# Attention's values of two groups by seven products of quarters, in a two-layer block on one core

## The chip, the cores and the metric

The kernel runs on one core of one Trainium2 chip. The metric is the device time of one execution, in microseconds (us); the lower the better. TensorE's matmul side is called PE here, its loading of the stationary operand PEld, VectorE DVE, ScalarE ACT, GpSimd POOL and SyncE SP.

## The reference: what is computed

Two layers run on 512 tokens of width 1024, in fp32. Layer 0 mixes tokens by a gated linear recurrence (HGRN2), layer 1 by dilated attention, and each ends in a feed-forward network (FFN). The change touches layer 1's attention. Its core in the reference:

```python
proj = (u @ w_in).reshape(B, S, N_GROUPS, 3, ATT_HEADS, ATT_HEAD_DIM)
for gi, (window, dilation) in enumerate(((128, 1), (512, 4), (2048, 16))):
    q = apply_partial_rope(proj[:, :, gi, 0], cos, sin) * scale
    k = apply_partial_rope(proj[:, :, gi, 1], cos, sin)
    v = proj[:, :, gi, 2]
    o_g, lse_g = dilated_group_attention(q, k, v, window, dilation)
```

Three groups of eight heads of 128 have their own queries, keys and values, each a product of u (512 x 1024) with 1024 columns of the weights; the three outputs are merged by a softmax over their log-sums. Group 1 attends in token order; groups 2 and 3 (1 and 2 in the code, which counts from 0) attend inside the four classes of tokens that are equal modulo four.

## The kernel before, in words

**Precision.** An fp32 value is kept as two fp32r parts, hi and lo (`uh`, `ul` for u; `hi`, `lo` or `hiq`, `loq` for weights). A product is three matmuls, hi by hi, lo by hi, hi by lo, issued by `three` (lines 408 to 410 of the kernel before, 428 to 430 of the changed one). Weights come from DRAM as fp32 in tiles `raw` of 128 x 2048 (1 MB), two at a time, on SP's queue; ACT casts a tile to hi (line 83), DVE subtracts to get lo (line 84). Three pairs of hi and lo exist. `Stream` holds the list of all loads of the program in the order of their use; the kernel's loops take from it in that order, and `weave` mixes in the loads of the adaptive-norm weights (`ada`), which DVE multiplies and sums (line 244).

**FFN.** It computes its products by seven products of quarters instead of eight. For these `token_sums` makes sums of token quarters (`th`, `tl`), POOL and DVE make sums of weight quarters (lines 772, 776, 780), and DVE combines the products out of PSUM (lines 817 to 832). Its matmuls have 256 columns.

**Attention.** `tok_proj` computes the values of one group and half of the columns (512): for each of four tiles of 128 tokens, eight tiles of 128 of the inner dimension, three matmuls of 512 columns, u stationary and the weights moving, 96 in all. For groups 2 and 3 the stationary tile takes each fourth token of u (`res`), so that V stands by classes. `block` computes queries or keys of one head and group with the weights stationary and all 512 tokens of u moving (24 matmuls of 512 columns); ACT evacuates them (`qk_evac`, line 1554), for groups 2 and 3 sorted into classes on the way, and copies the 32 rows that turn into `turning` (1555); DVE turns them (`turn_pair`, lines 1562 to 1565), ACT copies them back (1568), with a step for groups 2 and 3. Group 1's first half of values runs inside the FFN of layer 0 (`v_prod`), where it fills PE while the residual h and u are made. Then come groups 2 and 3, the pairs of heads 0 to 4, the second half of the values of all groups, and the pairs of heads 5 to 7. The softmax work of a head (`scores`, `merge`, `flip`, `pv`) is put at fixed numbers of blocks behind its pairs; `mixer_out` holds what is left of the last heads in its `tail`.

## Time and profile before

| | |
|---|---|
| median of 3 runs | 1522.97 us (1522.70 to 1523.41) |
| the profiled execution | 1522.93 us |
| its span, first to last instruction | 1521.0 us |
[...]
| busy: PE, DVE, ACT, POOL | 1506.4, 1024.8, 689.5, 234.9 us |
| DRAM read, written | 189.17 MB, 2.16 MB |

A profile shows one execution. Matmuls overlap, so what one of them costs is read from the distance between the starts of neighbours in the timeline, not from its length. "A <- B" in a wait reads: A waited, and B's end let it go. A line number is that of the helper that issued the instruction where a helper did.

### The profile page before, as it was taken

Reading aid. Unit: us, or ns where it says so; the run is one execution under the profiler, and the core shown is the slowest. Engines: PE = TensorE matmul, PEld = TensorE weight load, DVE = VectorE, ACT = ScalarE, POOL = GpSimd, SP = SyncE. Lnnn points to the kernel's source line nnn. Section 1 sums busy time; section 2 is a strip of 40 time slices with the busy share of each in tenths; the row PEclk is TensorE's granted clock in tenths of the full one; section 3 lists DMA queues with packets and bytes.
Section 4 is the critical chain, followed back from the end, with each engine's and each line's share of the span. In section 5 each row is a group of like instructions: output and inputs, shape, how many; then the busy total and the mean of one; then the engine's idle time right before and its main releaser. Section 6 shows DMA issues by size and latency. Waiting matters only on the chain.

```text
span 1521.0 us, 22710 instructions
## 1 busy us (share of the span) xinstructions
PE 1506.4 (99%) x8943; PEld 1325.7 (87%) x8943; DVE 1024.8 (67%) x1750; ACT 689.5 (45%) x1099; POOL 234.9 (15%) x208
## 2 busy tenths in 40 slices
PE   8999999999999999999999999999999999999998
PEld 6777888898999988889888888988888899999886
DVE  4587867487888897472567686335656978888633
ACT  4443433353444432362456664245645544544231
POOL 1011211031222212040010111000002212221100
PEclk9999999999999999999999999999999999999999
DMA  9654445125333366414544433433212333334521
GB/s 308 185 160 147 150 133 166 56 89 161 112 111 112 111 201 223 137 56 138 167 117 131 120 110 108 150 100 90 78 32 80 100 96 112 109 105 148 199 106 56
DMA packets 205498, 192.79 MB, mean 127 GB/s; under 512 B 6680, under 2 KB 164560, under 8 KB 205392
## 3 DMA queue, kind: packets, MB, share of 16 engines
q1 hardware_dynamic: 203856, 190.87, 40.9%
q8 instruction: 70, 1.15, 0.3%
q0 software_dynamic: 1024, 0.13, 0.2%
q10 hardware_dynamic: 512, 0.35, 0.1%
q14 instruction: 36, 0.29, 0.1%
HBM read 189.17 MB, written 2.16 MB: 126 GB/s over the span
## 4 chain that ended last, share of the span: by engine, by line
PE 93%; issue 2%; ACT 2%; POOL 1%; DVE 1%; DMA 1%; POOLq 0%; DVEq 0%; ACTq 0%
PE ps_mm L408 21%; PE ps_mm L410 20%; PE ps_mm L409 20%; PE ps_b L408 3%; PE ps_b L410 3%; PE ps_b L409 3%; PE ps_a L408 3%; PE ps_a L409 3%; PE ps_a L410 3%; PE ps_mm L1162 1%; ACT junk L444 1%; PE ps_a L1162 1%; PE ps_a L1607 1%; PE ps_a L1589 1%; PE ps_mm L222 1%
## 5 line engine op out<-in xcount | busy, mean ns | idle before, releaser
L408 PE MATMUL ps_mm<-uh,hi 128*128 128x512 f32 (+1 forms) x784 | 297.1, 379 | 0.0
L409 PE MATMUL ps_mm<-ul,hi 128*128 128x512 f32 (+1 forms) x784 | 294.9, 376 | 1.0 <-DVE ul L508 1.0
L410 PE MATMUL ps_mm<-uh,lo 128*128 128x512 f32 (+1 forms) x784 | 295.9, 377 | 0.0
L84 DVE TENSOR_TENSOR lo<-raw,hi 128x2048 fp32r<-128x2048 f32 x76 | 180.4, 2374 | 163.7 <-ACT hi L83 163.6
L83 ACT CAST hi<-raw 128x2048 fp32r<-128x2048 f32 x76 | 145.1, 1909 | 161.1 <-DMA raw<-in_ffn_w_out_dram 45.8
L408 PEld LDWEIGHTS ps_mm<-uh,hi 128*128 128x128 f32 x784 | 147.7, 188 | 34.2 <-issue 8.4
L409 PEld LDWEIGHTS ps_mm<-ul,hi 128*128 128x128 f32 x784 | 147.7, 188 | 26.4 <-DVE ul L508 1.4
L410 PEld LDWEIGHTS ps_mm<-uh,lo 128*128 128x128 f32 x784 | 147.6, 188 | 25.9
L788 ACT CAST hiq<-raw 128x1024 fp32r<-128x1024 f32 x68 | 68.3, 1050 | 65.7 <-DVE raw L776 64.7
L408 PE MATMUL ps_mm<-hi,oh 128*128 128x512 f32 x240 | 94.0, 392 | 0.0
L409 PE MATMUL ps_mm<-lo,oh 128*128 128x512 f32 x240 | 93.4, 389 | 0.0
L246 POOL PARTITION_ALL_REDUCE shared<-shared x14 | 46.4, 3312 | 281.3 <-DVE shared L244 281.2
L244 DVE SCALAR_TENSOR_TENSOR shared<-raw,cond,shared 128x512 f32<-128x512 f32 x98 | 73.2, 747 | 21.4 <-DMA raw<-in_ada_w_dram 19.9
L792 DVE TENSOR_TENSOR loq<-raw,hiq 128x1024 fp32r<-128x1024 f32 x68 | 80.0, 1217 | 0.4 <-ACT hiq L788 0.4
L410 PE MATMUL ps_mm<-hi,ul 128*128 128x512 f32 x192 | 75.9, 395 | 0.0
L409 PE MATMUL ps_mm<-lo,uh 128*128 128x512 f32 x192 | 75.9, 395 | 0.0
L408 PE MATMUL ps_mm<-hi,uh 128*128 128x512 f32 x192 | 74.5, 396 | 0.0
L772 POOL TENSOR_TENSOR raw<-raw 128x512 f32<-128x512 f32 x34 | 54.6, 1605 | 104.2 <-DVE loq L768 47.7
L410 PE MATMUL ps_mm<-hi,ol 128*128 128x512 f32 x176 | 68.5, 389 | 0.0
L776 DVE TENSOR_TENSOR raw<-raw 128x1024 f32<-128x1024 f32 x34 | 41.7, 1225 | 39.1 <-POOL raw L772 39.1
L408 PE MATMUL ps_a<-hi,oh 128*128 128x512 f32 x152 | 59.6, 392 | 0.0
L409 PE MATMUL ps_a<-lo,oh 128*128 128x512 f32 x152 | 59.2, 389 | 0.0
(402 smaller groups left out, 3813.3 us busy)
## 6 DMA issues: line engine op xcount, KB each, us to landing
raw<-in_ada_w_dram SPq DMA_DIRECT2D x40, 1024.0 KB, 5.2
raw<-in_ffn_w_in_dram SPq DMA_DIRECT2D x136, 256.0 KB, 4.3
raw<-in_attn_w_in_dram SPq DMA_DIRECT2D x48, 512.0 KB, 5.2
raw<-in_ffn_w_out_dram SPq DMA_DIRECT2D x22, 1024.0 KB, 4.9
raw<-in_hgrn_w_in_dram SPq DMA_DIRECT2D x12, 1024.0 KB, 5.5
raw<-in_attn_w_in_dram SPq DMA_DIRECT2D x12, 1024.0 KB, 5.1
raw<-in_ffn_w_in_dram SPq DMA_DIRECT2D x10, 1024.0 KB, 5.4
first<-in_ada_w_dram SPq DMA_DIRECT2D x14, 512.0 KB, 7.5
```

The source lines that it names most:

```text
L83: self.nc.scalar.copy(hi, t)
L84: self.nc.vector.tensor_sub(lo, t, hi.bitcast(F32))
L244: dve.scalar_tensor_tensor(a, r[:, k], sc, a, op0=OP.mult, op1=OP.add)
L246: pool.partition_all_reduce(a, a, P, bass.bass_isa.ReduceOp.add)
L408: pe.matmul(ps, ah, bh, start=start, stop=False)
L409: pe.matmul(ps, ah, bl, start=False, stop=False)
L410: pe.matmul(ps, al, bh, start=False, stop=stop)
L772: pool.tensor_add(r[:, 2], r[:, 2], r[:, 0])
L776: dve.tensor_tensor(r[:, 0:2], r[:, 0:3:2], r[:, 1:2].broadcast_to((P, 2, 512)), op=OP.add)
L788: act.copy(hi, src)
L792: dve.tensor_sub(lo, src, hi.bitcast(F32))
L1162: pe.matmul(vbanks[hf, t], a, w, start=e == 0 and which == 0, stop=e == KT - 1 and which == 2)
```

## The change

**Values.** Groups 2 and 3 use `seven_values`. A half of a group's columns is a product of 512 tokens x 1024 with 1024 x 512; it is cut into quarters (tokens, inner dimension and columns in two), and seven products of 256 tokens x 512 x 256 replace eight. Each product is two tiles of tokens x four inner tiles x three matmuls of 256 columns, 24; seven make 168. Four of them take sums or differences of u's quarters (`th`, `tl`), four sums or differences of the weights' quarters, which POOL (line 1389) and DVE (1390 to 1392) make in the raw tiles; ACT casts each quarter (1371), DVE subtracts (1372). ACT copies the first product into V (1418), DVE combines the other six (1426 to 1440). `prepare` steps the next group's weights while the present group's products run.

**u by classes.** u's two parts are also kept in the order of classes (`apart`, eight casts on ACT, line 1651, eight on DVE, 1652). Queries and keys use them, so that their evacuation is in place for groups 2 and 3 and has a step for group 1; the angles' table is sorted likewise. `th` and `tl` lie in the place of `uh` and `ul`, which nobody needs after group 1's values.

**Order.** Group 1's second half of values follows the first directly; it goes to DRAM (`v_away`) and comes back into V[0] after the second block of seven products. Then the pairs of group 1 and 2 of head 0, the first block (groups 2 and 3, first half), the third pair, heads 1 to 4, the second block, heads 5 to 7.

**Room.** The residual h goes to DRAM (`h_away`, 4 x 512 KB, at the end of FFN of layer 0, on ACT's queue) and comes back in `mixer_out`'s tail; its place holds the sums of tokens at first and then the softmax tiles `PN`, `PR` and `pt`. There is one tile `turning`, not two. The masks are made earlier, in V's room. The diff, cut:

```diff
-        at = []
-        order = []
-        for hd in range(NH):
-            if hd == 0:
-                for g in range(3):
-                    order.append(("v", g, 0))
-                    at += av(g, 0)
-            for g in range(3):
+        order, at = [], []
+        def values(hf, gs):
+            for g in gs:
+                order.append(("v", g, hf))
+                at.extend([("half", w[1]) for w in av(g, hf)])
+        def pairs(hd, gs=range(3)):
+            for g in gs:
                 order.append(("qk", g, hd))
                 at.append(aqk(g, hd))
-            if hd == 4:
-                for g in range(3):
-                    order.append(("v", g, 1))
-                    at += av(g, 1)
-        items += weave(at, ada_seq((1, 2), (1, 4), (1, 3)), 6, 2)
+        def woven(others, every):
+            items.extend(weave(at, others, 0, every))
+            at.clear()
+        for hf in range(2):
+            at += av(0, hf)
+        pairs(0, (0, 1))
+        values(0, (1, 2))
+        woven([], 1)
+        late = ada_seq((1, 2), (1, 4), (1, 3))
+        pairs(0, (2,))
+        for hd in range(1, 5):
+            pairs(hd)
+        woven(late[:8], 1.5)
+        values(1, (1, 2))
+        woven([], 1)
+        for hd in range(5, NH):
+            pairs(hd)
+        woven(late[8:], 1.3)
...
+                    for t in range(NT):
+                        act.dma_start(h_away[t], h[:, t])
...
-        def tok_proj(dst, c0, view, ticks=()):
+        def tok_proj(done):
             ws = [st.take(), st.take(1)]
             for t in range(NT):
                 ps = bank("mm")
+                tok = slice(t * P, (t + 1) * P)
                 for kt in range(KT):
                     whi, wlo = ws[kt // 4]
                     w = slice((kt % 4) * 512, (kt % 4 + 1) * 512)
-                    three(ps, view(uh[:, kt])[t], view(ul[:, kt])[t], whi[:, w], wlo[:, w], kt == 0, kt == KT - 1)
-                act.copy(dst[:, t, c0:c0 + 512], ps)
-                if t in ticks:
-                    fl.tick()
-        nat = lambda a: [a[:, t * P:(t + 1) * P] for t in range(NT)]
-        res = lambda a: [a.rearrange("p (l r) -> p r l", r=4)[:, t] for t in range(NT)]
...
+        def seven_values(dsts, apart, th, tl):
+            C = lambda raw, c: V4(raw)[:, :, c * 256:c * 256 + 256]
+            G = lambda t, o: V4(t[:, o * 1024:(o + 1) * 1024])
+            u_of = lambda r, c: lambda kt, n: [a[:, r * 4 + kt, c * 256 + n * P:c * 256 + (n + 1) * P] for a in apart]
+            t_of = lambda i: lambda kt, n: [a[:, i, kt, n * P:(n + 1) * P] for a in (th, tl)]
+            raws, tiles = {}, {}
+            def cut(i, tile, o, k, c):
+                hi, lo = tiles[i, tile]
+                src = C(raws[i][k], c)
+                act.copy(G(hi, o), src)
+                dve.tensor_sub(G(lo, o), src, G(hi, o).bitcast(F32))
+            def place(i, tile):
+                tiles[i, tile] = st.part_tiles()
+            def prepare(i, step):
+                if i >= len(dsts):
+                    return
+                if step == 0:
+                    raws[i] = [st.whole(), st.whole()]
+                    place(i, 0)
+                    cut(i, 0, 0, 0, 0)
+                    cut(i, 0, 1, 1, 1)
+                elif step == 1:
+                    place(i, 1)
+                    cut(i, 1, 0, 1, 0)
+                    a, b = raws[i]
+                    pool.tensor_add(C(b, 1), C(b, 1), C(a, 1))
+                    dve.tensor_add(C(a, 1), C(a, 1), C(a, 0))
+                    dve.tensor_add(C(a, 0), C(a, 0), C(b, 1))
+                    dve.tensor_add(C(b, 0), C(b, 0), C(a, 0))
+                    cut(i, 1, 1, 0, 0)
+                elif step == 2:
+                    place(i, 2)
+                    cut(i, 2, 1, 0, 1)
+                    cut(i, 2, 0, 1, 1)
+                else:
+                    place(i, 3)
+                    cut(i, 3, 0, 1, 0)
+                    raws.pop(i)
+                    st.fill()
+            def run(ps, i, tile, o, us):
+                hi, lo = tiles[i, tile]
+                for n in range(2):
+                    for kt in range(4):
+                        w = slice(o * 1024 + kt * 256, o * 1024 + (kt + 1) * 256)
+                        three(ps[:, n * 256:(n + 1) * 256], *us(kt, n), hi[:, w], lo[:, w], kt == 0, kt == 3)
+            H2 = lambda a: a.rearrange("p (n c) -> p n c", n=2)
+            for step in range(3):
+                prepare(0, step)
+            for i, dst in enumerate(dsts):
+                X, Y, Z, U = (dst[:, t:t + 2, c:c + 256] for c in (0, 256) for t in (0, 2))
+                m1 = bank("mm")
+                run(m1, i, 0, 0, u_of(0, 0))
+                act.copy(X, H2(m1))
+                m4 = bank("a")
+                run(m4, i, 0, 1, t_of(2))
+                prepare(i, 3)
+                m2 = bank("mm")
+                run(m2, i, 1, 0, u_of(1, 0))
+                m6 = bank("mm")
+                run(m6, i, 1, 1, t_of(3))
+                dve.tensor_add(Y, X, H2(m6))
+                dve.tensor_add(X, X, H2(m2))
+                prepare(i + 1, 0)
+                m5 = bank("mm")
+                run(m5, i, 2, 0, t_of(0))
+                m7 = bank("mm")
+                run(m7, i, 2, 1, t_of(1))
+                dve.scalar_tensor_tensor(Z, Y, -1.0, H2(m7), op0=OP.mult, op1=OP.subtract)
+                dve.tensor_add(Y, Y, H2(m5))
+                dve.tensor_sub(U, Z, H2(m5))
+                dve.tensor_sub(Z, Z, H2(m4))
+                prepare(i + 1, 1)
+                m3 = bank("mm")
+                run(m3, i, 3, 0, u_of(1, 1))
+                dve.tensor_add(Y, Y, H2(m3))
+                prepare(i + 1, 2)
...
+        def to_away(t, ps):
+            act.copy(V[1][:, t], ps)
+            if t == NT - 1:
+                act.dma_start(v_away, V[1])
...
+        PNs, PR_h = [h[:, k].rearrange("p (t n) -> p t n", t=4) for k in range(2)], h[:, 2].rearrange("p (t n) -> p t n", t=4)
...
+        apart = [up.tile([P, KT, S], F32R, name=f"apart{k}") for k in range(2)]
+        for kt in range(KT):
+            act.copy(V4(apart[0][:, kt]), L4(uh[:, kt]).bitcast(F32))
+            dve.tensor_copy(V4(apart[1][:, kt]), L4(ul[:, kt]).bitcast(F32))
+        tok_proj(to_away)
+        th, tl = (t.rearrange("p (a b) n -> p a (b n)", a=4).rearrange("p a (b n) -> p a b n", b=4) for t in (uh, ul))
+        token_sums(th, tl, h.rearrange("p t (a n) -> p (t a) n", a=2), *apart)()
...
-                pair.append(fresh(mk, [64, S], "turning", 2))
-            act.activation(*((tl, ps) if g == 0 else (V4(tl), L4(ps))), AF.Copy, scale=scale)
+                pair.append(fresh(mk, [64, S], "turning", 1))
+            act.activation(*((tl.rearrange("p (l r) -> p l r", r=4), R4(ps)) if g == 0 else (tl, ps)), AF.Copy, scale=scale)
...
-                act.copy(*((dst, src) if g == 0 else (V4(dst), L4(src))))
+                act.copy(*((dst.rearrange("p (l r) -> p l r", r=4), R4(src)) if g == 0 else (dst, src)))
...
-        for kind, g, i in order[1:]:
+        for kind, g, i in order:
             if kind == "v":
-                tok_proj(V[g], 0, nat if g == 0 else res, (0, 1, 2) if i and g == 0 else ())
+                if g == 1:
+                    seven_values(V[1:], apart, th, tl)
+                    if i:
+                        act.dma_start(V[0], v_away)
                 continue
...
-                ps = block(whi, wlo, k * D, P)
+                ps = block(whi, wlo, k * D, P, u=apart)
...
-        tail = {-1: [lambda: scores(7, 2), mkx.close], 2: [lambda: merge_r(7)], 3: [lambda: merge_n(7)],
-                4: [lambda: flips_r(7)], 5: [lambda: pv_r(7), lambda: flips_n(7)], 6: [lambda: pv_n(7)]}
+        upx.close()
+        tail = {-1: [lambda: scores(7, 2), mkx.close], 2: [lambda: merge_r(7), back(0)], 3: [lambda: merge_n(7)],
+                4: [lambda: flips_r(7)], 5: [lambda: pv_r(7), lambda: flips_n(7), back(2)], 6: [lambda: pv_n(7), back(1)],
+                7: [back(3)]}
```

Three places show how instructions move. First ACT, where the attention begins; `V` is the evacuated values, hi tiles the weights. Before:

```order
L104 CAST hi_6205<-raw_5815 128x1024 x2
L1522 COPY V_6089<-ps_mm_6213 128x512
L83 CAST hi_6297<-raw_5985 128x2048
L1522 COPY V_6089<-ps_mm_6239 128x512
L83 CAST hi_6303<-raw_6211 128x2048
L1334 COPY V_6090<-ps_mm_6310 128x512
```

Now, the casts into `apart` and the residual's DMAs stand between the last cast for group 1's first half and the evacuation of its last tiles:

```order
L105 CAST hi_6206<-raw_5816 128x1024 x2
L1050 DMA h_away<-h 128x1024 x4
L1651 CAST apart_6286<-uh 128x512 x8
L1626 COPY V_6090<-ps_mm_6219 128x512
L84 CAST hi_6304<-raw_5986 128x2048
L1626 COPY V_6090<-ps_mm_6245 128x512
L84 CAST hi_6311<-raw_6212 128x2048
```

What moved: the second tile of the next projection's weights (`hi_6304`) is cast behind eight more casts.

Second DVE, where it prepares weights for values. Before, at the first values of groups 2 and 3, each tile of weights is one subtraction, with adaptive-norm work between:

```order
L84 TENSOR_TENSOR lo_6298<-raw_5985,hi_6297 128x2048
L84 TENSOR_TENSOR lo_6304<-raw_6211,hi_6303 128x2048
L84 TENSOR_TENSOR lo_6415<-raw_6301,hi_6414 128x2048
L84 TENSOR_TENSOR lo_6421<-raw_6307,hi_6420 128x2048
L242 TENSOR_SCALAR shared<-raw_6418,cond 128x512
```

Now, in the first block, for group 3's sums of weights (`raw_6605`, `raw_6684` are its two raw tiles) among group 2's last combinations:

```order
L1440 TENSOR_TENSOR V_6091<-V_6091,ps_mm_6811 128x2x256
L1390 TENSOR_TENSOR raw_6605<-raw_6605 128x4x256
L1436 TENSOR_TENSOR V_6091<-V_6091,ps_a_6655 128x2x256
L1372 TENSOR_TENSOR loq_6838<-raw_6684,hiq_6837 128x1024
L1391 TENSOR_TENSOR raw_6605<-raw_6605,raw_6684 128x4x256
L1372 TENSOR_TENSOR loq_6838<-raw_6605,hiq_6837 128x1024
L1392 TENSOR_TENSOR raw_6684<-raw_6684,raw_6605 128x4x256
L1372 TENSOR_TENSOR loq_6802<-raw_6605,hiq_6801 128x1024
```

What moved: three sums of raw quarters and the subtractions that depend on them stand in one queue with the combinations.

Third POOL, at the end of layer 0's FFN; `rr` is the power that gives the root of the norm, which u of a token tile waits for. Before, the masks stand behind all of u; here from the fourth tile's root on:

```order
L459 TENSOR_TENSOR rr_6008<-rv_6006,expo 128x1
L459 TENSOR_TENSOR rr_6041<-rv_6039,expo 128x1
L508 TENSOR_TENSOR ul<-u_6029,uh 128x4x128
L508 TENSOR_TENSOR ul<-u_6034,uh 128x4x128
L459 TENSOR_TENSOR rr_6070<-rv_6068,expo 128x1
L459 TENSOR_TENSOR rr_6137<-rv_6135,expo 128x1
L508 TENSOR_TENSOR ul<-u_6139,uh 128x4x128
L508 TENSOR_TENSOR ul<-u_6144,uh 128x4x128
L508 TENSOR_TENSOR ul<-u_6191,uh 128x4x128
L508 TENSOR_TENSOR ul<-u_6196,uh 128x4x128
L1534 MEMSET zero 128x128
L1540 IOTA lq 128x128
L1535 AFFINE_SELECT maskN<-zero 128x128
L1538 AFFINE_SELECT maskN<-zero 128x128
L1538 AFFINE_SELECT maskR<-zero 128x128
```

Now:

```order
L479 TENSOR_TENSOR rr_6009<-rv_6007,expo 128x1
L1658 MEMSET V_6092 128x128
L1663 IOTA V_6092 128x128
L1659 AFFINE_SELECT maskN<-V_6092 128x128
L1662 AFFINE_SELECT maskN<-V_6092 128x128
L1662 AFFINE_SELECT maskR<-V_6092 128x128
L479 TENSOR_TENSOR rr_6042<-rv_6040,expo 128x1
L528 TENSOR_TENSOR ul<-u_6030,uh 128x4x128
```

What moved: the five operations of the masks stand before the root of the third token tile (`rr_6042`).

## Rows read from the trace of the kernel before

**Rows 1.** The page's first part: busy time of each engine, share of the span, instructions

```profile
PE 1506.4 (99%) x8943; PEld 1325.7 (87%) x8943; DVE 1024.8 (67%) x1750; ACT 689.5 (45%) x1099; POOL 234.9 (15%) x208
```

**Rows 2.** Waits of PE in the attention: engine, line, releaser; total us, times, longest

```profile
PE ps_b L1691 <- ACT pt L1660: 1.7, 1, 1.7
```

**Rows 3.** Stretch, us, busy us (and count) of PE, PEld, DVE, ACT, POOL; clock, DMA share

```profile
700.00:727.00 27.00, 27.00 (x116) 27.00 (x116) 7.32 (x6) 8.27 (x8) 0.00 (x0) 1.00 0.41 117
800.00:900.00 100.00, 100.00 (x533) 85.89 (x533) 74.89 (x230) 64.43 (x112) 13.44 (x13) 1.00 0.44 122
```

**Rows 4.** Timeline of PE, strided values: start, length, line, operation, out<-in

```profile
700.50 0.39 PE L408 MATMUL ps_mm<-hi,uh 128*128 128x512 f32 x1
...
723.06 0.39 PE L408 MATMUL ps_mm<-hi,uh 128*128 128x512 f32 x1
```

**Rows 5.** Timeline of PE in the second FFN, matmuls of 256 columns

```profile
1243.15 0.28 PE L408 MATMUL ps_mm<-th,hiq 128*128 128x256 f32 x1
...
1246.55 0.28 PE L408 MATMUL ps_mm<-th,hiq 128*128 128x256 f32 x1
...
1246.89 0.28 PE L408 MATMUL ps_mm<-uh,hiq 128*128 128x256 f32 x1
...
1249.51 0.28 PE L409 MATMUL ps_a<-ul,hiq 128*128 128x256 f32 x1
```

**Rows 6.** Groups of stationary loads (PEld), whole span: busy us, mean ns | idle

```profile
L410 PEld LDWEIGHTS ps_mm<-hi,ul 128*128 128x128 f32 x192 | 51.6, 269 | 2.5
...
L408 PEld LDWEIGHTS ps_mm<-th,hiq 128*128 128x128 f32 x204 | 38.4, 188 | 0.0
```

**Rows 7.** Timelines of ACT and of PE at the start of the attention

```profile
674.34 2.00 ACT L104 CAST hi<-raw 128x1024 fp32r<-128x1024 f32 x2
...
683.34 0.40 PE L409 MATMUL ps_mm<-lo,uh 128*128 128x512 f32 x1
```

**Rows 8.** Timeline of ACT at the last heads

```profile
1116.56 1.08 ACT L1683 COPY oT_late<-ps_b 128x512 f32<-128x512 f32 x1 [2.73 <-PE ps_b L1682]
1117.67 2.24 ACT L1568 COPY qk<-turning 32x512 f32<-32x512 f32 x2
```

**Rows 9.** Groups of instructions in the second FFN, 1190 to 1400

```profile
L792 DVE TENSOR_TENSOR loq<-raw,hiq 128x1024 fp32r<-128x1024 f32 x36 | 42.3, 1217 | 0.0
L788 ACT CAST hiq<-raw 128x1024 fp32r<-128x1024 f32 x36 | 36.2, 1050 | 32.5 <-DVE raw L776 31.7 <-DVE raw L780 0.8
L772 POOL TENSOR_TENSOR raw<-raw 128x512 f32<-128x512 f32 x18 | 29.4, 1631 | 56.2 <-DVE loq L768 27.5 <-DVE spare L768 15.1 <-DMA raw<-in_ffn_w_in_dram 13.6
...
L776 DVE TENSOR_TENSOR raw<-raw 128x1024 f32<-128x1024 f32 x18 | 22.0, 1225 | 19.7 <-POOL raw L772 19.7
...
L821 DVE TENSOR_TENSOR shared<-shared,ps_a 128x512 f32<-128x512 f32 x9 | 6.1, 680 | 0.6 <-ACT shared L861 0.6
```

**Rows 10.** Timelines of POOL and of DVE around the masks

```profile
662.05 0.55 POOL L459 TENSOR_TENSOR rr<-rv,expo 128x1 f32<-128x1 f32 x1 [3.00 <-DVE rv L457]
...
676.60 0.20 POOL L1534 MEMSET zero<- 128x128 f32 x1
...
677.74 1.26 POOL L1538 TENSOR_SCALAR_AFFINE_SELECT maskN<-zero 128x128 f32<-128x128 f32 x1
678.96 0.29 POOL L1538 TENSOR_SCALAR_AFFINE_SELECT maskR<-zero 128x128 f32<-128x128 f32 x1
...
675.42 3.43 DVE L105 TENSOR_TENSOR lo<-raw,hi 128x1024 fp32r<-128x1024 f32 x2 [1.92 <-ACT hi L104]
```

**Rows 11.** DMA issues in the attention: count, KB each, median us to landing

```profile
raw<-in_attn_w_in_dram SPq DMA_DIRECT2D x48, 512.0 KB, 5.2
...
raw<-in_attn_w_in_dram SPq DMA_DIRECT2D x9, 1024.0 KB, 5.1
```

**Rows 12.** Groups of instructions in the attention, 655 to 1160

```profile
L84 DVE TENSOR_TENSOR lo<-raw,hi 128x2048 fp32r<-128x2048 f32 x35 | 82.2, 2348 | 106.6 <-ACT hi L83 106.6
...
L1568 ACT COPY qk<-turning 32x512 f32<-32x512 f32 x48 | 45.3, 944 | 25.8 <-DVE turning L1565 22.5 <-DVE wZ L1633 2.7
```

46 lines of the change are left out of this document (27 added, 19 removed).

## The prediction

> **What bounds the kernel now.** I read the busy times first: TensorE (PE) is busy for 1506.4 of 1521.0 us, the next engine, VectorE (DVE), for 1024.8 [rows 1]. Then PE's waits in the attention: one only, 1.7 us [rows 2]. Then the stretches: while the strided value projections run (700 to 727) PE is full and DVE has 7.32 us of work in 27; while the query/key pairs run (800 to 900) PE is full and DVE has 74.89 in 100, ScalarE (ACT) 64.43 [rows 3]. So time falls only if PE gets less to do, and only as far as what feeds it keeps up. The profiled execution took 1522.93 us, its span of 1521.0 and 1.93 around it; the median of the runs, 1522.97, is 0.04 from it, so I work against 1522.93.
>
> **The change, part by part.** *The products.* Now four value projections (groups 2 and 3, two halves of columns) issue 96 matmuls of 512 columns each, with tokens read at a step of four as the stationary side. Two of these matmuls, 96 apart, start at 700.50 and 723.06 [rows 4]: 22.56 / 96 = 0.2350 us each. All: 4 x 96 x 0.2350 = 90.2 us. After it, each projection is 7 products x 24 matmuls = 168 of 256 columns. The feed-forward network (FFN) has such matmuls at two speeds [rows 5]: with th moving, 30 between 1243.15 and 1246.55, 0.1133 us; with uh moving, 22 between 1246.89 and 1249.51, 0.1191 us. That gives 4 x 168 x 0.1133 = 76.1 or x 0.1191 = 80.0. The moving side is now the weights' tiles. The program places them at the same offset within 512 bytes as uh (192; th stands at 128), the one thing in which I see them nearer to one row than to the other, so I take 0.1191: **10.2 us less**; the other end is 14.1 less.
>
> Does it hurt that a load of the stationary side now serves 256 columns and not 512? A strided load takes 269 ns on average, one of th's products 188 [rows 6], which is more than 0.1133, and the matmuls follow each other at 0.1133 all the same; so these loads are hidden there, and I add nothing. [...]
>
> *Start of attention.* ACT gets eight casts of u into the order by fours, DVE eight more and five sums, before the weights that group 1's second half of values needs. The first half's last matmul is over at 683.3, where the next projection begins now [rows 7]; in the new order some 20 matmuls of the second half then run on the weights' first tile, until about 688, before the second tile's hi is needed. ACT has ended its earlier casts at 676.3 [rows 7]; two of its strided small copies take 2.24 us [rows 8], so eight are 9.0, one evacuation 0.6, the cast 2.1 (twice L788 [rows 9]): 688.0. DVE starts at 675.4 [rows 10] with the subtractions of 2.35 us that it has now, its eight casts (0.68 each, as the 128x512 operation in [rows 9]) end at 683.2, the five sums of 1.22 (as L776 [rows 9]), which wait for ACT's casts too, at about 691, lo at 693.5; it is needed some 25 matmuls after hi, at 694. These sums also wait for the residual's 2 MB to leave for DRAM: 512 KB lands in 5.2 us [rows 11]. Margins of half a microsecond; I take 0.5 lost, ends 0 and 2.
>
> *Preparation inside a block of seven products.* For one group's half: eight casts on ACT (1050 ns each), eight subtractions (1217), three sums (1225) and seven combinations out of PSUM (0.68) on DVE, one sum of 128x1024 on POOL, twice L772's 1631 ns [rows 9]. DVE: 9.7 + 3.7 + 4.8 = 18.2 us, beside 168 x 0.1191 = 20.0 us of PE. It fits, but narrowly, where now a projection asks two subtractions of 2.35 us each [rows 12]. What ends last in the first block is group 3's fourth product (m6). Counting from the first seven-product matmul, with nothing lost: group 2's m4 ends at 6.6 (with 0.9 for the scores woven in), its last cut frees the second raw buffer at 6.6 + 1.05 + 1.22 = 8.9, the load lands at 14.1, casts and subtractions end at 17, POOL's sum at 20.2, DVE's first sum at 21.4, a subtraction and the second sum at 23.9, ACT's casts and DVE's third sum, in order behind one evacuation, end at 27, its lo at 29. PE asks for it at 20.0 + 0.9 + 8.6 + 0.8 = 30.3. Margin 1.3 us, and each hop between engines, not counted, takes a part of it. I take 1.5 lost there and at the first query/key pair behind the block (its weights' buffer is freed by the same chain: load 5.2, cast 2.1, subtraction 2.35, some 3 us before they are needed), ends 0 and 5. In the second block group 2's weights are long in; I take 0.5, ends 0 and 2.
>
> *The tail.* The 1.7 us wait is PE's for pt, which ACT makes behind a strided copy (1.08) and two more (2.24) [rows 8]. In the new order of tokens these two copies are contiguous. Of the 48 of their line 32 are strided now; at 1.12 each they leave (45.3 - 35.8) / 16 = 0.6 for a contiguous one [rows 12], so the two are 1.0 less. **1.0 us gained**, ends 0 and 1.7.
>
> *Covered edits.* Group 1's evacuations become the strided ones instead of two groups': less work on ACT, which isn't late. One buffer for turning instead of two: ACT's next evacuation waits for two copies behind 2.8 us of DVE, while a pair's 48 matmuls of 512 columns hold PE for 10.9 us (twice 0.1133 each) and have several banks; nothing, unless DVE is late by over 3 us. The residual comes back in four parts of 512 KB, 5.2 us each [rows 11], asked for between the last heads' products, and is read only after the output projection's second half; nothing, and at worst one landing, 5.2. Group 1's values go out and back (1 MB each way) under query/key pairs, where no one asks for them; nothing. The adaptive-norm weights come each 1.5 pairs instead of each 2 and use up some of the 25 us in 100 that DVE has free [rows 3]; nothing, and B if that is wrong.
>
> *The masks.* POOL's five operations move into FFN's tail, in front of the reciprocal root at 662.05, where POOL had idled 3.00 us; now they run from 676.60 to 679.25, 2.65 us. One select of two alike took 1.26 us and the other 0.29, while DVE's pair of subtractions took 3.43 [rows 10] instead of the 2.35 of as many columns [rows 12]: POOL and DVE hold each other up there. I take 0, ends 0 and 1: the gap is as long as the operations. [...]
>
> *Sum.* 1522.93 - 10.2 + 0.5 + 1.5 + 0.5 - 1.0 = **1514.2 us**.
>
> **The rivals.** *A. The matmuls go at 0.1133.* For it: stationary loads and tile sizes are those of th's rows. Against it: the moving side's place. 14.1 + 1.0 less, and 4 lost in starvation, as the cover shrinks by 1 us a group: 1511.8.
>
> *B. DVE falls behind in the blocks.* 18.2 of 20.0 us is full use; turning a query/key pair (four operations of some 0.7) and the maxima of the scores come on top in the first block, and what is late there is late for the pairs behind. Against it: half of group 2's preparation is done before the block. Priced at the 2.8 of one turning and some hops, 3 us more in each block: 1520.2.
>
> *C. The raw buffers starve PE (slower).* Both raw buffers must come free, be filled and be summed before a fourth product. With a landing of x us instead of 5.2 the fourth product stalls by about x - 6.5, the next pair by x - 8.5, in two blocks: 4x - 30. It eats the gain of 8.7 + 2 when x passes 10 and is slower beyond 0.2% from x = 11; at x = 11.5 it loses 16, 1522.93 - 11.2 + 16 + 0.5 = 1528.2. For it: the two loads go out close together, as the residual and group 1's values use the same DMA engines. Against it: all loads of this kind land in 5.1 to 5.2 us [rows 11] while the engines are 41 to 44% busy [rows 3].
>
> *D. Loads of the stationary side show.* If each narrow matmul waits for its load's 188 ns: 4 x 168 x 0.188 = 126.3 instead of 80.0, 46.3 more: 1560.5. The rows of FFN speak against it. [...]
>
> **How the numbers follow.** Forecast 0.51 (its own range 1512 to 1518), A 0.17, B 0.20, C 0.09, D 0.03. A measurement of this kernel tells 0.2%, 3 us, from no change. Faster by more: the forecast, A and half of B, 0.78; within: the other half of B and a part of C, 0.12; slower: the rest of C and D, 0.10. The range runs from 1509.5, below A with 2 us less of waiting, to 1521.0, past B.
>
> **What would show it.** Of the changed kernel: seven-product matmuls start 0.119 us apart (0.113 in A, 0.19 in D); each block of 336 lasts 40 to 42 us; PE's waits name the sum of weights (line 1391) or a cast behind it for 1 to 2 us in the first block and little in the second (B: DVE over 90% busy in both; C: DMA of raw as what ends the waits); the wait at pv_n of the last heads is 0.7 us or less. The prediction is wrong if PE's count of products is right and the time stays over 1521, or if a wait of more than 3 us stands at a place not named here.

## The result: slower by 0.3%, and the profile after

The changed kernel takes 1528.02 us (median of 7 runs, 1526.11 to 1530.65), the kernel before 1523.41 in the same job (7 runs). The ratio is 1.003, 95% interval 1.0018 to 1.0041: slower, where 1514.2 was forecast. The profiled execution took 1529.39 us, its span 1527.7; PE's mean granted clock over it, 1 being full speed, was 0.996, before 0.999.

The page's first part of the changed kernel, as [rows 1]:

```profile
PE 1502.0 (98%) x9231; PEld 1318.2 (86%) x9231; DVE 1084.8 (71%) x1830; ACT 701.1 (46%) x1119; POOL 248.4 (16%) x212
```

PE is busy for 4.4 us less, and the span is 6.7 longer. Waits of PE in the attention of the changed kernel, 655 to 1168, as [rows 2]:

```profile
PE ps_a L1710 <- ACT qk L1689: 3.4, 2, 1.9
PE ps_a L1728 <- ACT qk L1689: 2.4, 1, 2.4
PE ps_mm L428 <- ACT hiq L1371: 2.1, 1, 2.1
PE ps_b L1815 <- DVE h L1784: 1.3, 1, 1.3
PE ps_b L1813 <- ACT h L1782: 0.7, 1, 0.7
PE ps_a L1777 <- DVE sN L1715: 0.5, 1, 0.5
PE ps_a L1777 <- DVE h L1772: 0.5, 1, 0.5
PE ps_b L1804 <- ACT h L1782: 0.4, 1, 0.4
```

11.3 us in place of 1.7. Stretches of the changed kernel, columns as in [rows 3]:

```profile
750.00:760.00 10.00, 10.00 (x86) 10.00 (x85) 9.26 (x9) 4.25 (x5) 2.40 (x1) 1.00 0.00 0
760.00:770.00 10.00, 7.91 (x54) 7.72 (x54) 6.77 (x14) 2.09 (x2) 0.00 (x0) 0.83 0.44 115
830.00:840.00 10.00, 8.45 (x49) 7.17 (x49) 5.56 (x8) 4.76 (x6) 4.15 (x2) 1.00 0.77 207
840.00:850.00 10.00, 7.80 (x31) 6.70 (x32) 7.10 (x35) 5.56 (x13) 0.59 (x2) 0.83 0.41 110
727.00:776.00 49.00, 45.36 (x356) 44.70 (x355) 32.59 (x51) 21.35 (x29) 4.05 (x3) 0.97 0.28 87
956.00:1002.00 46.00, 45.59 (x384) 45.40 (x383) 29.58 (x41) 19.39 (x25) 3.92 (x3) 1.00 0.37 117
```

Around the two longest waits the granted clock is 0.83 over 10 us: it is 0.50 from 764 to 767 and from 843 to 845, 1.00 from 762 to 763 and from 846 to 847. Matmuls of 256 columns, 0.120 us apart from 768 on, start 0.213 us apart between 763.79 and 766.99. My estimate of the loss is (1 - 0.83) x 10 = 1.7 us of work, twice. The kernel before lost none in its attention (1.00 from 655 to 1168).

**An account.** I measure the attention from PE's first transposition of the normed input (about 656) to the first of `mixer_out`'s (about 1160), in the profiled executions, and take PE's waits and the clock's loss off. Before: 505.23 - 1.68 = 503.55 us of work. The change: 510.94 - 11.30 - 3.4 = 496.2. So the products did give 7.3 us; waits and clock took 14.7. The remaining 0.8 us of the difference of 6.5 arose ahead of the attention. Profiles here differ by more than that: over all kernels the attention's start spreads over 3.1 us.

**Where the waits come from.** Two of the waits behind the first block, followed back in the timelines of the changed kernel. First SP, which issues the weight loads, DVE, and ACT:

```profile
801.53 6.99 SPq L64 DMA_DIRECT2D raw<-in_attn_w_in_dram  x4
```

```profile
798.42 3.08 DVE L85 TENSOR_TENSOR lo<-raw,hi 128x2048 fp32r<-128x2048 f32 x1 [1.45 <-ACT hi L84]
...
837.38 0.49 DVE L245 TENSOR_SCALAR shared<-raw,cond 128x512 f32<-128x512 f32 x1 [2.76 <-DMA raw<-in_ada_w_dram]
...
840.12 0.68 DVE L1686 TENSOR_TENSOR turning<-turning,rot 64x512 f32<-64x512 f32 x1
```

```profile
807.59 1.91 ACT L84 CAST hi<-raw 128x2048 fp32r<-128x2048 f32 x1 [6.35 <-DMA raw<-in_attn_w_in_dram]
809.40 2.22 ACT L1689 COPY qk<-turning 32x512 f32<-32x512 f32 x2
...
840.88 1.26 ACT L1689 COPY qk<-turning 32x512 f32<-32x512 f32 x2 [6.09 <-DVE turning L1686]
```

and PE:

```profile
811.68 1.79 PE L1710 MATMUL ps_a<-qk,qk 128*128 128x128 f32 x8 [1.87 <-ACT qk L1689]
...
842.20 2.02 PE L1728 MATMUL ps_a<-qk,qk 128*128 128x128 f32 x8 [2.42 <-ACT qk L1689]
```

DVE's subtraction frees a raw buffer at 801.50, SP issues the next load at 801.53, and ACT, idle for 6.35 us, casts it at 807.59. Behind that cast in ACT's queue stands the copy of rows that DVE had turned by 805.21; PE's scores wait for the copy until 811.68. At 837.38 it is DVE that stands 2.76 us before an adaptive-norm tile, with the turning of a pair queued behind; ACT copies at 840.88, PE goes on at 842.20. **PE doesn't wait for the late tile, but for small work that stands behind it in a queue.** Waits of ACT from 770 to 850 say the same of the whole stretch:

```profile
ACT hi L84 <- DMA raw<-in_attn_w_in_dram: 29.1, 6, 8.2
ACT qk L1689 <- DVE turning L1686: 6.6, 2, 6.1
```

In the kernel before no cast of that stretch waits for a load; one issued at 781.09 there is cast at 790.66, 9.6 us later, with landings of 5.2 [rows 11]. A late cast alone costs nothing, though: behind the second block of the changed kernel one waits for its load for 8.23 us (1006.49), and PE waits 0.69 us in that whole stretch.

The two waits in the first block have another origin. PE, DVE, SP and ACT of the changed kernel there:

```profile
727.26 0.28 PE L428 MATMUL ps_mm<-hiq,apart 128*128 128x256 f32 x1
...
731.36 1.79 PE L1710 MATMUL ps_a<-qk,qk 128*128 128x128 f32 x8 [1.55 <-ACT qk L1689]
...
738.37 0.28 PE L430 MATMUL ps_a<-hiq,ul 128*128 128x256 f32 x1
...
762.51 0.50 PE L428 MATMUL ps_mm<-hiq,uh 128*128 128x256 f32 x2 [2.09 <-ACT hiq L1371]
```

```profile
726.09 1.21 DVE L1392 TENSOR_TENSOR raw<-raw,raw 128x1024 f32<-128x1024 f32 x1
727.22 1.22 DVE L1372 TENSOR_TENSOR loq<-raw,hiq 128x1024 fp32r<-128x1024 f32 x1
728.36 0.68 DVE L1686 TENSOR_TENSOR turning<-turning,rot 64x512 f32<-64x512 f32 x1
...
742.18 1.23 DVE L1372 TENSOR_TENSOR loq<-raw,hiq 128x1024 fp32r<-128x1024 f32 x1 [3.62 <-ACT hiq L1371]
...
760.17 1.21 DVE L1391 TENSOR_TENSOR raw<-raw,raw 128x1024 f32<-128x1024 f32 x1
...
770.04 0.69 DVE L1426 TENSOR_TENSOR V<-V,ps_mm 128x512 f32<-128x512 f32 x1 [3.27 <-PE ps_mm L430]
```

```profile
743.48 0.37 SPq L66 DMA_DIRECT2D raw<-in_attn_w_in_dram  x1
```

```profile
741.11 2.23 ACT L1371 CAST hiq<-raw 128x1024 fp32r<-128x1024 f32 x2
749.66 2.00 ACT L1371 CAST hiq<-raw 128x1024 fp32r<-128x1024 f32 x2 [6.33 <-DMA raw<-in_attn_w_in_dram]
```

At 731.36 PE waits for turned rows of head 0: a sum and a subtraction of the block's preparation (726.09, 727.22) stand on DVE before the last step of the turning. At 762.51 it waits for m6's weights. Group 2's last cut, which frees the second raw buffer, ends at 743.41; SP issues the load at once, it is cast at 749.66, and from 750.74 DVE has no pause until 766.77 (3.27 us before 770.04). So line 1391's sum ends only at 761.38, and the cast behind it lets PE go at 762.51.

### The profile page after: what moved, and what is told of

Same layout as the page of the kernel before. It is cut to its first block, busy times and chain, and to the rows that moved or that the text cites. A ratio compares the mean times of both kernels' runs of the same rounds, so it can differ in the third digit from the quotient of the medians.

```text
span 1527.7 us, 23466 instructions
## 1 busy us (share of the span) xinstructions
PE 1502.0 (98%) x9231; PEld 1318.2 (86%) x9231; DVE 1084.8 (71%) x1830; ACT 701.1 (46%) x1119; POOL 248.4 (16%) x212
## 3 DMA queue, kind: packets, MB, share of 16 engines
q0 software_dynamic: 1024, 0.13, 0.2%
## 5 line engine op out<-in xcount | busy, mean ns | idle before, releaser
L430 PE MATMUL ps_mm<-apart,lo 128*128 128x512 f32 x384 | 151.7, 395 | 0.0
L429 PE MATMUL ps_mm<-apart,hi 128*128 128x512 f32 x384 | 151.4, 394 | 0.0
L428 PE MATMUL ps_mm<-apart,hi 128*128 128x512 f32 x384 | 150.4, 392 | 0.0
L428 PE MATMUL ps_mm<-uh,hi 128*128 128x512 f32 (+1 forms) x400 | 146.3, 366 | 0.0
L429 PE MATMUL ps_mm<-ul,hi 128*128 128x512 f32 (+1 forms) x400 | 144.3, 361 | 1.0 <-DVE ul L528 1.0
L430 PE MATMUL ps_mm<-uh,lo 128*128 128x512 f32 (+1 forms) x400 | 144.5, 361 | 0.0
L428 PEld LDWEIGHTS ps_mm<-uh,hi 128*128 128x128 f32 x400 | 75.5, 189 | 19.7 <-issue 8.4
L429 PEld LDWEIGHTS ps_mm<-ul,hi 128*128 128x128 f32 x400 | 75.6, 189 | 12.1 <-DVE ul L528 1.5
L430 PEld LDWEIGHTS ps_mm<-uh,lo 128*128 128x128 f32 x400 | 75.5, 189 | 11.4
L428 PEld LDWEIGHTS ps_mm<-apart,hi 128*128 128x128 f32 x384 | 72.4, 189 | 14.7
L430 PEld LDWEIGHTS ps_mm<-apart,lo 128*128 128x128 f32 x384 | 72.5, 189 | 14.3
L429 PEld LDWEIGHTS ps_mm<-apart,hi 128*128 128x128 f32 x384 | 72.3, 188 | 14.4
```

Source lines behind the costliest of these rows:

```text
L428: pe.matmul(ps, ah, bh, start=start, stop=False)
L429: pe.matmul(ps, ah, bl, start=False, stop=False)
L430: pe.matmul(ps, al, bh, start=False, stop=stop)
```

## The experiments

Each is compared with the kernel before in its own job (medians 1522.87 to 1524.97 us).

**1. The adaptive-norm loads later.** They begin three pairs later, one each 1.25 pairs. `woven` gets a third argument for it, the pair behind which its loads begin; some later experiments use it too.

```diff
-        woven(late[:8], 1.5)
+        woven(late[:8], 1.25, 3)
```

> Edit: the eight adaptive-norm loads of heads 0 to 4 begin behind the fourth query/key pair after the first block (first = 3, one each 1.25 pairs) instead of behind the first (one each 1.5); the same loads, the same products. Theory L (lost lead): while a block of seven products runs, both raw buffers are held, the pairs' weights can't be loaded ahead, and the adaptive-norm loads that follow at once keep the lead from being rebuilt, so that ACT's casts wait for raw (29.1 us in 770 to 850 in the changed kernel, none in the kernel before) and the small copies behind them in ACT's queue make PE wait (1.87, 0.47, 1.32 and 2.42 us). L expects these four waits gone or below 1 us together, 6 to 8 us less with the clock they cost: 1520 to 1522.5. Theory D (density): DVE is too full wherever adaptive-norm work stands at one load in 1.5 pairs; denser at 1.25, the waits move 30 us later and stay 4 to 7 us: 1526 to 1530. Theory B (the blocks): the loss lies in the blocks, this edit changes nothing: 1527 to 1529.

1527.46 us, ratio 1.0027 (1.0018 to 1.0037). The waits of 1.87 and 2.42 behind the block are gone, one of 3.46 us stands at 829.16 (PE at line 1803 for DVE's h): moved, not removed, as theory D had it.

**2. Fewer in the first heads.**

```diff
-        woven(late[:8], 1.5)
+        woven(late[:6], 2)
...
-        woven(late[8:], 1.3)
+        woven(late[6:], 1.1)
```

> Edit: in heads 0 to 4 six adaptive-norm loads, one each two pairs from the first pair on, in heads 5 to 7 six instead of four, one each 1.1 pairs. Theory L (lost lead): still a load at once behind the block, so the first waits stay in part: 3 to 5 us less than the changed kernel, 1523 to 1525. Theory D (density): at the density of the kernel before the waits of the first stretch go, and new ones come behind the second block, where it is denser now: 1522 to 1527, PE's waits between 1000 and 1100 over 2 us (0.7 in the changed kernel). Theory B (the blocks): no change, 1527 to 1529.

1528.24 us, 1.0036 (1.0023 to 1.0049). The time is theory B's, but not for B's reason, that nothing changes: 2.9 us of waits between 821 and 839 stand in place of 6.1 between 811 and 843, and 3.38 are new at 1073.72, where the loads now stand closer, as D had it.

**3. Eight products again**, with all else of the change kept, adaptive-norm loads too (`tok_proj` now gets its tokens as an argument).

```diff
-                at.extend([("half", w[1]) for w in av(g, hf)])
+                at.extend(av(g, hf))
...
-                    seven_values(V[1:], apart, th, tl)
+                    for k in (1, 2):
+                        tok_proj(lambda t, ps: act.copy(V[k][:, t], ps), apart)
```

> Edit: groups 2 and 3 have their values from 96 matmuls of 512 columns each again, with the tokens by classes (contiguous) as the stationary side; order, loads, room and the sums of tokens stay as changed, seven products and their sums of weights are gone. All theories: 4 x 96 x 0.2267 = 87.1 us of products against 82.8 in the changed kernel. Theory L (lost lead): weights go through the stream as before, the lead is kept, all waits between 727 and 850 go (9.7 us and some 3 of clock): 1528.0 + 4.3 - 12 = 1520, so that seven products cost more than they give. Theory D (density): the adaptive-norm work is unchanged, the waits at 811 to 842 stay: 1526 to 1529. Theory B (the blocks): the waits in the block go (3.6), those behind stay: 1528.

1518.07 us, 0.997 (0.9959 to 0.9981): faster than both. PE waits nowhere in the attention, which lasts 500.25 us, 3.3 less work than before: that is the stationary side read in a row instead of at a step, 0.2267 us from one matmul to the next instead of 0.2350, 384 x 0.0083 = 3.2. So the closer adaptive-norm loads, the single turning buffer and the traffic to DRAM cost PE no wait as long as the blocks of seven products are not there.

**4. The third pair of head 0 before the first block.**

```diff
-        pairs(0, (0, 1))
+        pairs(0)
...
-        pairs(0, (2,))
```

> Edit: all three pairs of head 0 stand ahead of the first block, not two; the block ends where head 1 begins. Theory L (lost lead): the wait on the sum of weights in the block (2.1 us) stays, the waits behind it stay and touch head 1's pairs: 1526 to 1529. Theory D: the same, 1526 to 1529. Theory B (the blocks): the block's own waits, 1.55 for the scores of head 0 and 2.1 for the sum of weights, come from preparation that starts too late after the start of attention; one pair more (10.9 us) ahead of it takes them away: 1523 to 1525.

1521.55 us, 0.9988 (0.998 to 0.9997). The block has no wait left; 2.43 at 834.28 and 1.55 at 878.31 stay. Waits are 5.49 and the clock's loss 1.7: 8.4 us of attention less for the move of one pair. Theory B named the cause and had it too small (1523 to 1525): more time ahead of the block takes its own waits away.

**5. POOL's sum of weights on DVE.**

```diff
-                    pool.tensor_add(C(b, 1), C(b, 1), C(a, 1))
+                    dve.tensor_add(C(b, 1), C(b, 1), C(a, 1))
```

> Edit: the one sum of weight quarters that POOL makes (3.31 and 2.40 us in the first block, while one of DVE's subtractions beside it took 3.11 instead of 1.22) is made by DVE, four sums in all. Theory P (the chain of sums starves the block): the chain is some 2 us shorter, the waits inside the first block (1.55 on the copies behind DVE's turning, 2.09 on the sum's cast) shrink to under 1 us together, those behind it stay: 1523.5 to 1526. Theory F (DVE is too full in the block): DVE has 1.2 us more per group, the waits stay: 1527 to 1530.

1520.61 us, 0.9985 (0.9976 to 0.9994), better than was expected. What POOL's sum did is read in the changed kernel's timelines of POOL and DVE:

```profile
752.10 2.40 POOL L1389 TENSOR_TENSOR raw<-raw,raw 128x1024 f32<-128x1024 f32 x1 [7.08 <-DVE loq L1372]
```

```profile
750.74 1.23 DVE L1372 TENSOR_TENSOR loq<-raw,hiq 128x1024 fp32r<-128x1024 f32 x1 [4.87 <-ACT hiq L1371]
...
752.48 3.11 DVE L1372 TENSOR_TENSOR loq<-raw,hiq 128x1024 fp32r<-128x1024 f32 x1
```

The same subtraction takes 1.23 us alone and 3.11 beside POOL's sum, and is done 1.1 us after it. With the sum on DVE the wait at m6 shrinks from 2.09 to 0.94, the one before it from 1.55 to 1.28. Waits are still 9.28, but no stretch of the attention is below full clock (mean over the span 0.998, 0.996 in the change), so the 3.4 lost to the clock come back as well. That makes 5.4 us between the two profiled executions; this kernel's median lies 3.3 below its profiled one (1523.94), and no profile shows why.

**6 and 7. Seven products in one block only**, in the second (`if i:`; in the values' list `if hf`) and in the first (the opposite).

```diff
-                    seven_values(V[1:], apart, th, tl)
+                    if i:
+                        seven_values(V[1:], apart, th, tl)
+                    else:
+                        for k in (1, 2):
+                            tok_proj(lambda t, ps: act.copy(V[k][:, t], ps), apart)
```

> Edit: eight products (96 matmuls of 512 columns, contiguous stationary) for the first half of the values of groups 2 and 3, seven products for the second half only. Against the kernel with eight products in both (1518.1): Theory 1 (the first block's place costs: it stands at the start of the attention and is followed by adaptive-norm loads at one in 1.5 pairs): the second block has waits of 0.5, 0.4 and 0.7 us behind it in the changed kernel, saves 2 x (96 x 0.2267 - 168 x 0.1200) = 3.2 us, and the time is 1515 to 1517. Theory 2 (seven products cost more than they give wherever they stand): half of the 10 us between the two kernels comes back, 1521 to 1524.

> Edit: the complement of the kernel with seven products in the second half only: seven in the first block, eight in the second. Theory 1 (place): all of the loss comes back with the first block, 1518.1 - 3.2 + 9.7 of waits + 3 of clock = 1527 to 1529. Theory 2 (wherever they stand): half, 1521 to 1524.

The second alone: 1523.22 us (1519.21 to 1525.05, wide; 1520.54 in the profile), 1.0 (0.9991 to 1.0009); no wait before the block, 0.95, 1.19 and 2.37 us at 951, 992 and 1043. The first alone: 1528.63 us, 1.0037 (1.0025 to 1.005), waits in and behind the first block (1.52, 1.77, 1.66, 0.46, 0.49, 0.92, 2.43), none behind the second. Each block brings its own waits, the first most of them. Neither theory holds for both kernels: against experiment 3 the second block alone costs 5.2 us, the first alone 10.6, both together 10.0.

**8. Three edits together:** 4, 5, and the adaptive-norm loads from the third pair on.

```diff
-        pairs(0, (0, 1))
+        pairs(0)
...
-        pairs(0, (2,))
...
-        woven(late[:8], 1.5)
+        woven(late[:7], 1.5, 2)
...
-        woven(late[8:], 1.3)
+        woven(late[7:], 1.2)
...
-                    pool.tensor_add(C(b, 1), C(b, 1), C(a, 1))
+                    dve.tensor_add(C(b, 1), C(b, 1), C(a, 1))
```

> Edit: seven products in both blocks with three edits together: all three pairs of head 0 ahead of the first block, the sum of POOL on DVE, and the adaptive-norm loads of heads 1 to 4 from the third pair behind the block on, seven instead of eight, the rest one each 1.2 pairs behind the second block. Theory 1 (place): with 1521.6 for the first edit alone, the two waits left there (2.43 and 1.55, with their clock some 5 us) shrink: 1516 to 1519. Theory 2 (seven products cost wherever they stand) and theory F (DVE too full): waits come back at other places, 1520 to 1524.

**1513.76 us**, 0.9941 (0.9928 to 0.9953): the best kernel here, and about the time that was forecast for the change itself, by chance (15). Its attention lasts 495.02 us with one wait:

```profile
PE ps_b L1803 <- ACT h L1781: 0.4, 1, 0.4
```

ACT's casts of this kernel wait for loads only up to 795.97, then run ahead of them until the second block:

```profile
795.97 1.91 ACT L84 CAST hi<-raw 128x2048 fp32r<-128x2048 f32 x1 [2.01 <-DMA raw<-in_attn_w_in_dram]
803.76 1.89 ACT L84 CAST hi<-raw 128x2048 fp32r<-128x2048 f32 x1
819.11 1.91 ACT L84 CAST hi<-raw 128x2048 fp32r<-128x2048 f32 x1
```

**9 to 12. Which of the three does it?** The other combinations of the edits of 8: head 0 first (H), sum on DVE (S), the loads from the third pair on (A). g1 is 8 without A, g2 without S, g3 without H; g4 is A alone:

```diff
-        woven(late[:8], 1.5)
+        woven(late[:7], 1.5, 2)
...
-        woven(late[8:], 1.3)
+        woven(late[7:], 1.2)
```

> Edit: two of the three edits of the 1513.8 us kernel: all pairs of head 0 ahead of the first block, and POOL's sum of weights made by DVE; the adaptive-norm loads as in the change. So far against the change (1528.0): head 0 first 6.5 less, sum on DVE 7.4 less, all three edits 14.2 less. Theory T (two separate starvations, one before the block by too late a start, one in it by POOL's sum): the two add up, 1513.5 to 1515, waits of PE in the attention under 1 us. Theory A (the adaptive-norm loads right behind the block are a third one): two waits behind the block stay, 1516 to 1519.

> Edit: head 0's pairs ahead of the first block and the later adaptive-norm loads; POOL keeps its sum of weights. Theory T: without the edit of the sum the time stays near that of head 0 first alone (1521.6): 1519 to 1522. Theory A: the waits behind the block go, 1515 to 1518, and POOL's sum is worth little once it has time.

> Edit: POOL's sum made by DVE and the later adaptive-norm loads; the first block stands behind two pairs of head 0 as in the change. Theory T: near the sum on DVE alone (1520.6): 1518.5 to 1521. Theory A: the four waits behind the block (5.3 us in the profile of the sum alone) go, 1514.5 to 1517.5, and the two in the block (1.3 and 0.9) stay.

> Edit: the later adaptive-norm loads alone (seven, from the third pair behind the first block on, one each 1.5 pairs; the rest one each 1.2 pairs behind the second block). Theory T: little, as the two other ways to thin them (0.6 us less, 0.2 more): 1526 to 1529, the waits in the block stay. Theory A: the waits behind the block (6.1 us, and 3.4 of clock) go: 1519 to 1523.

| edits | us, median | us, profiled | ratio, 95% interval | PE's waits in the first block | behind it | clock's loss |
|---|---|---|---|---|---|---|
| none (the change) | 1528.02 | 1529.39 | 1.0030 (1.0018 to 1.0041) | 3.64 | 7.66 | 3.4 |
| H | 1521.55 | 1521.55 | 0.9988 (0.9980 to 0.9997) | 0 | 5.49 | 1.7 |
| S | 1520.61 | 1523.94 | 0.9985 (0.9976 to 0.9994) | 2.22 | 7.06 | 0 |
| A | 1529.60 | 1529.79 | 1.0040 (1.0027 to 1.0053) | 3.32 | 8.05 | 1.7 |
| H, S | 1526.38 | 1527.08 | 1.0018 (1.0009 to 1.0027) | 0 | 7.99 | 3.4 |
| H, A | 1520.23 | 1520.48 | 0.9979 (0.9970 to 0.9988) | 0 | 5.32 | 3.4 |
| S, A | 1531.88 | 1532.39 | 1.0054 (1.0041 to 1.0067) | 2.33 | 10.68 | 5.1 |
| H, S, A | 1513.76 | 1513.76 | 0.9941 (0.9928 to 0.9953) | 0 | 0.41 | 0 |

Waits and clock are those of the profiled execution; the clock's loss counts a slow stretch whole, also where it lies in a wait. H, A came within theory T's range and A 0.6 us above it, the other two as no theory had them: H and S gain 6.5 and 7.4 us alone and 1.6 together. The work, waits and clock taken off, stays at 493.6 to 496.6 us in all eight; only the waits differ. Inside the first block the edits do what they were made for, in every combination: with H no wait is left there, with S about a third of them goes. Behind it they don't add up. As an edit there shifts where loads fall, this is argued rather than shown for each combination.

**13 and 14. No adaptive-norm load before the second block.** In the change, and with H and S; the fourteen loads (twelve tiles of weights, two of biases) follow in heads 5 to 7.

```diff
-        woven(late[:8], 1.5)
+        woven([], 1)
...
-        woven(late[8:], 1.3)
+        woven(late, 0.6)
```

> Edit: the change with no adaptive-norm load in heads 0 to 4; all of them stand behind the second block (one each 0.6 pairs, more than two a pair is room for, so that stretch is expected to be slow; only the stretch from the first to the second block is read). Theory R (raw buffers): the waits between the blocks come from loads: two raw buffers, refilled in one order, and an adaptive-norm load in hand holds one of them while its four operations wait in DVE's queue; whatever stands behind a late load on ACT's or DVE's queue is late too. Without these loads PE's waits between 776 and 950 are gone (six of them, 7.2 us, in the change), those in the block (1.55 and 2.09) stay, and no cast waits for raw by more than 3 us behind the first two pairs. Theory S (seven products leave DVE and ACT behind, for some 60 us): waits of 2 us or more stay at 811 to 842.

> Edit: the kernel of 1526.4 us (head 0 first, sum on DVE) with no adaptive-norm load in heads 0 to 4, all behind the second block, as above. Theory R: its waits of 2.40, 0.72 and 4.12 us at 835, 861 and 882 are gone, and none stays before the second block. Theory S: at least one over 1 us stays there.

1539.62 us, 1.0101 (1.0085 to 1.0116), and 1533.56, 1.0061 (1.0047 to 1.0074). The times are those of the last heads, which now have all these loads; what was asked is the stretch between the blocks. In the change PE waits 6.1 us between 776 and 950, in four waits (the expectation had six and 7.2); without those loads, nothing. No cast of weights then waits for its load between 780.21 and the second block; the last one:

```profile
780.21 1.91 ACT L84 CAST hi<-raw 128x2048 fp32r<-128x2048 f32 x1 [4.64 <-DMA raw<-in_attn_w_in_dram]
```

With H and S 7.2 us (2.40, 0.72 and 4.12) up to 960 become 0.55. In the kernel without H and S the waits in the first block stay, with 1.50 and 2.19 us. Between the blocks it is the adaptive-norm loads; inside the block it isn't.

**15. The best kernel with these loads one pair later.**

```diff
-        woven(late[:7], 1.5, 2)
+        woven(late[:7], 1.5, 3)
```

> Edit: the kernel of 1513.8 us with the seven adaptive-norm loads one pair later (from the fourth pair behind the block on). Theory R with luck of phase: whether a late load meets a small copy that PE needs depends on where it falls; one pair later brings a wait or two back, 1516 to 1524. Theory M (margin): with three pairs ahead and the shorter sum the block leaves margin enough, 1513 to 1515.5.

1533.66 us, 1.0064 (1.0052 to 1.0077): 19.9 us slower than kernel 8 (18.7 by the ratios to the kernel before, which was slower in this job), worse than any theory had it. PE waits 14.6 us in the attention and the clock's loss is 5.1; one wait of 4.98 stands at 1053, behind the second block. Waits of PE from 776 to 950, where kernel 8 has none:

```profile
PE ps_a L1727 <- ACT qk L1688: 5.4, 2, 2.9
PE ps_a L1709 <- ACT qk L1688: 2.7, 2, 2.4
```

The longest of these in this kernel's timeline of DVE, then of POOL and PE:

```profile
862.40 1.54 DVE L247 SCALAR_TENSOR_TENSOR shared<-raw,cond,shared 128x512 f32<-128x512 f32 x2 [4.47 <-DMA raw<-in_ada_w_dram]
863.85 2.28 DVE L85 TENSOR_TENSOR lo<-raw,hi 128x2048 fp32r<-128x2048 f32 x1
...
869.08 2.72 DVE L1684 TENSOR_TENSOR turning<-turning,shared 64x512 f32<-64x512 f32 x1
```

```profile
868.66 3.59 POOL L249 PARTITION_ALL_REDUCE shared<-shared  x1 [4.03 <-DVE shared L247]
```

```profile
873.92 1.16 PE L1727 MATMUL ps_a<-qk,qk 128*128 128x128 f32 x8 [2.87 <-ACT qk L1688]
```

DVE stands 4.47 us before an adaptive-norm tile, the pair's lo and turning come late, and one step of the turning takes 2.72 us instead of 0.68 beside POOL's reduction of the same weights. So kernel 8 is fast by a lucky phase of its loads; this shift, the only one tried, finds no margin.

## Why the prediction was wrong, point by point

**The step that failed** stands under the covered edits: "The adaptive-norm weights come each 1.5 pairs instead of each 2 and use up some of the 25 us in 100 that DVE has free; nothing, and B if that is wrong." I judged the cover by DVE's idle share. What ran out is the lead of the loads. There are two raw buffers, filled in one order; a block keeps both until its last cut, so the pairs behind it are loaded as late as their buffer allows, and each adaptive-norm tile then holds one of the two until its DVE operations are through. Without the blocks the same loads cost nothing (experiment 3); without the loads, the block causes no wait behind it (13). It takes both: 6.1 us of waits where I had put nothing. That the buffers are the link is read from the chains above and from the casts, which wait 29.1 us for loads in the change and stop waiting after 780.21 in 13. But leaving the loads out takes their work on DVE and POOL away as well, and no run separates the two.

B's sign, DVE over 90% busy in both blocks, did not come: the changed kernel's DVE was busy for 32.59 of 49 us (727 to 776) and 29.58 of 46 (956 to 1002). Yet in the first block what B describes did happen: both waits there stand behind DVE, which from 750.74 to 766.77 had no pause.

**Against the forecast** the profiled time is 15.2 us over: 8.1 of waits beyond the 3.2 that the forecast's terms leave (0.5 + 1.5 + 0.5 + 0.7), 3.4 of clock, 2.8 of work, 0.8 ahead of the attention. Of the 8.1, 6.1 stand behind the first block and 2.1 in it. Term by term:

- *Products, 10.2 less.* Right in mechanism and nearly in size. In the changed kernel's timeline of PE

```profile
739.21 0.28 PE L428 MATMUL ps_mm<-hiq,uh 128*128 128x256 f32 x1
...
747.85 0.28 PE L428 MATMUL ps_mm<-hiq,apart 128*128 128x256 f32 x1
```

  are 72 matmuls apart: 8.64 / 72 = 0.1200 us, for which 0.1191 was taken; 672 x 0.1200 = 80.6, so 9.6 less. A (0.1133) and D (0.188) fall. Half the columns took half the spacing, 0.1200 us against 0.2350 before. That the tiles' place decides between 0.1133 and 0.1191, by which I chose, no run shows. Of the attention's work 7.3 us went in the change, 8.9 in kernel 8 and 7 to 10 in the others of the table; what the missing 2 us are I can't name. From their first matmul to their last the blocks lasted 48.2 and 46.5 us, not 40 to 42: scores and other small products stand in them, more than that sign allowed for, and in the first the waits.
- *Start, 0.5 lost.* PE did not wait there. ACT's eight casts took 8.3 us (9.0 forecast), DVE's 4.4 (5.4).
- *First block, 1.5 lost in it and at the next pair.* The wait at m6 came, named by the cast behind the sum, with 2.09 us; another 1.55 at 731.36, for the head's turned rows, was not foreseen, and none of the 6.1 us after 776 either. The chain that I counted "with nothing lost" was late from its start: the last cut was due 8.9 us after the block's first matmul and ended 16.2 after it, as m4 ended 4.8 us later than forecast and ACT came to the cut's cast 2.5 us after that. The first block's bound of 5 us took in only what one chain does to itself, not the pairs that inherit its lateness. The sum on POOL was priced at 3.2 us and took 2.4 to 3.3; that it would hold up DVE's subtraction for 1.9 us I had written of the masks only. Beside POOL's sum the subtraction took 3.11 us against 1.23; beside POOL's reduction in experiment 15 a step of the turning took 2.72 against 0.68 and ended 0.45 us before the reduction's recorded end. Experiment 5 shows what the sum was worth here.
- *Second block, 0.5.* 0.48 and 0.41 at 952 and 958, and 0.69 later, at 1052.
- *Tail, 1.0 gained.* The wait of [rows 2] is gone, 1.7.
- *h to DRAM and back, group 1's values, one turning buffer, masks: nothing.* Right, by experiment 3 as a whole.
- *C* named the raw buffers, which had their part in it, but priced them by a landing time over 11 us. Loads landed in 5.2 to 5.6 (medians, 5.1 and 5.2 before); what mattered was when they could be issued.

**The clock** was in no term. In the change stretches at 0.83 stood around the waits of 2.09 and 2.42 us and took, by the estimate above, 1.7 us each, so these two cost nearly double.

**Open:** which load falls behind which instruction in each of the combinations. Two chains were followed in the change and one in the shifted kernel; that the others behind the first block go by the same mechanism is argued from them. A third raw buffer, which would test it directly, was not tried.

## What to carry to other kernels

Where two streams of loads share a small ring of buffers, ask of a change not only whether the engines have free time, but how far ahead of its use each load is issued, and what small urgent work stands in the queue behind the instruction that will wait for it. If moving a load by one step changes the time by 20 us, single edits can't be judged by their single effects: give the ring its lead back, or try the edits together. And a sum handed to an idle POOL was not free here: a subtraction of DVE's beside it took 3.11 us instead of 1.23.

## What the runs showed of the hardware that was not expected

Waits of much the same length did not all cost clock: stretches of 10 us at a granted 0.83 stand around waits of 2.09 and 2.42 us in the changed kernel and of 2.36 and 2.53 us in experiment 15; around that kernel's wait of 2.87 us, from 870 to 880, the granted clock is 1.00. Beside POOL's reduction over partitions a DVE step was longer too, as the subtraction was beside POOL's sum: 2.72 us beside a reduction of 3.59 (experiment 15), where the same step takes 0.68 alone. And a reduction was longer beside DVE's work: in the changed kernel one that started at 902.88, while a subtraction of 2.29 us ran, took 5.34 us; the median of the kernel's fourteen is 3.25.
